# Mixer of a two-block network: the last conditioning blocks as a thread of their own, the first two parts of the output product as one, masked scans, and early priorities anew

## The chip, the cores and the metric

The kernel runs on one core of a Trainium2 chip. The metric is the device time of one launch in microseconds (us). Before the change it is 1557.97 us, the median of 3 runs (1557.44 to 1559.53). The engines are named as the profile names them: PE (TensorE matmul), PEld (its weight load), DVE (VectorE), ACT (ScalarE), POOL (GpSimd) and SP (SyncE, which only issues transfers here).

## The reference, cut to what matters

There are 512 tokens with 1024 features. The first block is the one that the change touches:

```python
ada = silu(c) @ w_ada + b_ada                 # 1024 -> 6 x 1024
sh_m, sc_m, g_m, sh_f, sc_f, g_f = split(ada, 6)
h = rms_norm(x) * (1 + sc_m) + sh_m
proj = h @ w_in                               # 1792 columns for RWKV, 512 for S5
z = shift(proj[..., :1792]); u = proj[..., 1792:]
y_rwkv = rwkv7_time_mix(z, ...)               # 8 heads of 64, a recurrence over the tokens
y_s5 = s5_mix(u, ...)                         # state space, GLU product, norm
x = x + g_m * (concatenate([y_rwkv, y_s5]) @ w_out)
h = rms_norm(x) * (1 + sc_f) + sh_f
x = x + g_f * ((silu(h @ w_gate) * (h @ w_up)) @ w_down)
```

Two hybrid layers (latent attention, short convolution, window attention) follow. The change only reaches them through the numbers that order some of their weight loads.

## The kernel before

**Products.** A large product is made of parts of 128 output features by 512 tokens. Each factor of 32 bits is split into a high and a low half, and three matmuls (high by high, high by low, low by high) of 128x512 make one k-tile of 128 rows. The weights' high half (`whi`) comes from ACT, the low half (`wlo`) from POOL or DVE. A part's sum lies in one of the three PSUM banks named `mm`; the job's evacuation reads it and frees it.

**The order.** Nothing of the mixer's order stands in the code. `class Flow` (from L378) runs threads, which are Python generators that yield one operation at a time. `Flow.run` always emits the operation with the earliest planned start, to which the thread's number in the table `BIAS` (L73) is added; this fixes every engine's program. The large products of the mixer are one fill thread, `gemm_g` (L1776), which walks through the list `JOBS` (L74 to L76): `z` (14 tiles of `h @ w_in`), `g` (the GLU product), `x` (the S5 half of `w_out`, four k-tiles, 8 jobs), `A` (two conditioning groups), then the RWKV half of `w_out` as `a` (two k-tiles, 8 jobs), `b` and `c` (one k-tile each, 8 jobs each). `a`, `b`, `c` wait for `mix.backs` > 1, > 2, > 3, the number of finished pairs of heads. Each job of `x`, `a`, `b`, `c` ends with `evac_x` (L1840): one DVE operation `xres += g_m * sum`.

**RWKV.** It goes over four pairs of heads p = 0 to 3. For each there are `front_a` (L1162, elementwise work and eight scans of 64 tokens), `front_b`, `invert` (a triangular inverse by way of transfers on SP's queue), `solve`, `chain` and `norm`. `chain` (L1416) is eight serial steps on one state: two matmuls from `UV` into columns 128:192 of the PSUM bank `cz`, two DVE operations that make the new state `Z`, one matmul from `Z` into columns 0:128, one DVE addition that makes the next `UV`. The matmuls into `Y` are the outputs of the step. `norm` (L1458) normalises `Y` and splits the result into `mr` (high and low), the factor of `a`, `b` and `c`.

**Conditioning.** The 48 blocks of `w_ada` are 12 groups. `group_a` (L1626) sums a group by 8 matmuls 32x512 (`<-wa,cT`), an ACT copy (`ev`), four matmuls 128x1 and one addition into `ada`. Ten groups run early; groups 10 and 11 (`g_f`, needed at the end of the FFN) are the jobs `A`. `finish` (L1907) closes the mixer when all 12 groups are there.

Of the kernel before, what the change touches and what calls it, by code (L numbers as in the profile page):

```python
# [47 lines left out]
_CR_SIZES = [("maskA", 128), ("mx", 64), ("i64", 64), ("blk", 128), ("sel0", 64), ("sel1", 64)]  # L48
# [38 lines left out]
LBIAS = {"latents": -2.98, "rows": -0.79, "token": 1.41, "keys": 1.03, "swa_q": 0.91, "head_gates": -0.43, "conv": -0.42, "mla_q": -0.75, "mla_k": -0.52, "mla_s": -2.46, "mla_m": -2.11, "mla_e": 1.23, "mla_n": 2.12, "mla_t": 1.14, "mla_v": -2.74, "swa_s": -1.25, "swa_m": 0.19, "swa_e": -2.03, "swa_v": -1.32, "convert": -0.49, "products": 1.27}  # L87
# [13 lines left out]
def _consts():  # L101
# [3 lines left out]
    c["ones"] = np.ones((128, 1))  # L105
    c["blkc"] = (p[:, None] // 64 == np.arange(2)[None]).astype(float)
# [31 lines left out]
def _tiles(w, kt, n):  # L138
    K, N = w.shape
    return np.ascontiguousarray(w.reshape(kt, 128, N // n, n).transpose(2, 1, 0, 3))  # L140


def pack(i):
# [9 lines left out]
    o["wada"] = np.concatenate([o.pop("wss"), wr], 0)  # L153
# [20 lines left out]
    o["wout"] = _tiles(np.concatenate([g["w_out"][0][:512], g["w_out"][0][512:][p5]], 0), 8, 128)  # L174
# [951 lines left out]
class Mix:  # L1126
# [35 lines left out]
    def front_a(self, p):  # L1162
# [371 lines left out]
def mixer(X, top, stop):  # L1534
# [115 lines left out]

    def loada(i0, i1, pool_, queue, bufs):
# [1285 lines left out]
```

## Time and profile before

| | us |
|---|---|
| median of 3 runs | 1557.97 (1557.44 to 1559.53) |
| the profiled execution | 1560.24 |
| its span | 1558.5 |
| PE busy | 1469.8 (94%) |
| DVE busy | 860.4 (55%) |
| ACT busy | 653.4 (42%) |
| POOL busy | 533.5 (34%) |

The profiled execution is 2.27 us above the median and 1.74 us longer than its span. Its mean granted clock of TensorE is 0.986. The mixer is the stretch from 0 to some 450 us; what follows is the FFN and the two layers.

How to read the rows below: a row of the timeline has the start, the duration, engine, line, operation, output<-inputs, the shape and the count of instructions that it holds, and in brackets how long the engine was idle just before and what ended that. A matmul's duration reaches from its start to its modelled end, so neighbouring ones overlap; the distance of starts says what one costs.

### The profile page before, as it was taken

How to read it: one execution, taken by the hardware profiler on the slowest of the kernel's cores; microseconds unless marked ns; L12 is line 12 of the kernel's file. 1: busy time of each engine (PE TensorE's matmuls, PEld its weight loads, DVE VectorE, ACT ScalarE, POOL GpSimd, SP SyncE). 2: the span in 40 equal slices, each digit the busy share in tenths (PEclk: the TensorE clock that was granted, in tenths of full speed). 3: DMA queues.
4: the chain of work that ended last, by engine and by line, in shares of the span. 5: the costliest groups of instructions: out<-in, count | busy, mean ns of one | idle time of the engine just before them, and what ended most of it. 6: DMA issues, size and time to landing. Idle time of an engine off the chain costs nothing.

```text
span 1558.5 us, 23572 instructions
## 1 busy us (share of the span) xinstructions
PE 1469.8 (94%) x8772; PEld 1123.0 (72%) x8772; DVE 860.4 (55%) x2011; ACT 653.4 (42%) x1316; POOL 533.5 (34%) x498
## 2 busy tenths in 40 slices
PE   4998899998879999999999989999999989999998
PEld 2666676666457888888888867866778867876776
DVE  6858776784676222221126474455874475463882
ACT  3422643232144333333333565355554366356452
POOL 1112350330323333334442454532325354542332
PEclk9999999999999999999999999999999999999999
DMA  6874141232222223333332311321222311221213
GB/s 251 288 214 90 50 121 32 70 94 75 63 82 75 97 95 98 98 95 91 98 95 63 103 55 54 102 68 55 71 54 88 91 61 61 81 76 61 70 54 102
DMA packets 97684, 141.92 MB, mean 91 GB/s; under 512 B 40977, under 2 KB 44945, under 8 KB 97553
## 3 DMA queue, kind: packets, MB, share of 16 engines
q1 hardware_dynamic: 90512, 120.46, 25.6%
q0 software_dynamic: 5760, 18.88, 3.9%
q8 instruction: 69, 1.13, 0.3%
q10 hardware_dynamic: 1296, 1.07, 0.2%
q14 instruction: 47, 0.38, 0.1%
HBM read 135.39 MB, written 4.98 MB: 90 GB/s over the span
## 4 chain that ended last, share of the span: by engine, by line
PE 74%; DVE 15%; ACT 4%; issue 2%; DMA 2%; POOL 1%; SPq 0%; ACTq 0%; DVEq 0%; POOLq 0%
PE mm L255 54%; PE rp L255 10%; PE rp L553 2%; PE O L255 2%; PE rq L255 2%; PE acc L255 2%; PE cz L255 1%; DVE wlo L236 1%; DVE sc L236 1%; DVE sq L236 1%; DVE P L249 1%; DVE qp L236 1%; POOL wlo L236 1%; DVE cy L252 1%; ACT qp L233 1%
## 5 line engine op out<-in xcount | busy, mean ns | idle before, releaser
L236 POOL TENSOR_TENSOR wlo<-wraw,whi 128x512 fp32r<-128x512 f32 (+2 forms) x300 | 379.6, 1267 | 766.4 <-ACT whi L233 731.1
L233 ACT ACTIVATE whi<-wraw 128x512 fp32r<-128x512 f32 (+2 forms) x392 | 239.1, 613 | 429.9 <-PE mm L255 300.7
L255 PE MATMUL mm<-hhi,wlo 128*128 128x512 f32 x920 | 368.4, 400 | 6.1 <-DVE wlo L236 6.1
L255 PE MATMUL mm<-hhi,whi 128*128 128x512 f32 x920 | 368.7, 401 | 1.7 <-DVE ca L236 1.0
L255 PE MATMUL mm<-hlo,whi 128*128 128x512 f32 x920 | 368.0, 400 | 0.0
L255 PEld LDWEIGHTS mm<-hhi,wlo 128*128 128x128 f32 x920 | 175.1, 190 | 49.5 <-DVE wlo L236 8.1
L255 PEld LDWEIGHTS mm<-hlo,whi 128*128 128x128 f32 x920 | 174.7, 190 | 44.0 <-issue 9.6
L255 PEld LDWEIGHTS mm<-hhi,whi 128*128 128x128 f32 x920 | 174.9, 190 | 42.6 <-issue 7.5
L236 DVE TENSOR_TENSOR wlo<-wraw,whi 128x512 fp32r<-128x512 f32 (+1 forms) x92 | 73.9, 804 | 113.7 <-ACT whi L233 102.9
L255 PE MATMUL mm<-ylo,whi 128*128 128x512 f32 x224 | 89.2, 398 | 1.6 <-POOL ylo L236 1.6
L255 PE MATMUL mm<-yhi,whi 128*128 128x512 f32 x224 | 89.7, 400 | 0.0
L255 PE MATMUL mm<-yhi,wlo 128*128 128x512 f32 x224 | 89.6, 400 | 0.0
L255 PE MATMUL mm<-ahi,whi 128*128 128x512 f32 x176 | 69.3, 394 | 0.0
L255 PE MATMUL mm<-ahi,wlo 128*128 128x512 f32 x176 | 69.0, 392 | 0.0
L255 PE MATMUL mm<-alo,whi 128*128 128x512 f32 x176 | 68.3, 388 | 0.0
L553 DVE CUSTOM_DVE_ANT_0 P<-rp,c,nsq 128x128 f32<-128x128 f32 (+1 forms) x64 | 34.2, 549 | 45.4 <-PE rp L255 41.3
L252 DVE SCALAR_TENSOR_TENSOR xres<-mm,ada,xres 128x512 f32<-128x512 f32 x40 | 29.7, 747 | 48.3 <-PE mm L255 48.1
L252 DVE SCALAR_TENSOR_TENSOR g<-th,mm 128x512 f32<-128x512 f32 x21 | 14.4, 687 | 70.6 <-PE mm L255 70.6
L252 DVE SCALAR_TENSOR_TENSOR th<-th,mm 128x512 f32<-128x512 f32 x20 | 13.7, 687 | 69.9 <-ACT th L233 69.9
L236 DVE TENSOR_TENSOR xres<-xres,mm 128x512 f32<-128x512 f32 x48 | 32.5, 681 | 35.0 <-PE mm L255 34.8
L255 PEld LDWEIGHTS mm<-ylo,whi 128*128 128x128 f32 x224 | 42.1, 188 | 12.5 <-POOL ylo L236 2.3
L255 PEld LDWEIGHTS mm<-yhi,wlo 128*128 128x128 f32 x224 | 42.0, 188 | 10.1 <-issue 1.1
(548 smaller groups left out, 2632.1 us busy)
## 6 DMA issues: line engine op xcount, KB each, us to landing
wraw<-in_w2m SPq DMA_DIRECT2D x124, 256.0 KB, 2.7
wa<-in_wada SPq DMA_DIRECT2D x40, 512.0 KB, 4.9
wraw<-in_wo SPq DMA_DIRECT2D x48, 256.0 KB, 2.7
wraw<-in_wgate SPq DMA_DIRECT2D x44, 256.0 KB, 2.7
wraw<-in_wup SPq DMA_DIRECT2D x44, 256.0 KB, 2.8
wraw<-in_wdown SPq DMA_DIRECT2D x40, 256.0 KB, 2.7
wraw<-in_wz POOLq DMA_DIRECT2D x24, 256.0 KB, 3.2
wa<-in_wada POOLq DMA_DIRECT2D x8, 512.0 KB, 3.7
```

Of the source, the lines that this page charges most:

```text
L233: return self.act.activation(out=out, in_=in_, func=func, **kw)
L236: return (eng or self.dve).tensor_tensor(out=out, in0=a, in1=b, op=op)
L249: return self.dve.tensor_scalar(out=out, in0=a, scalar1=s1, scalar2=s2, op0=op0, **kw)
L252: return self.dve.scalar_tensor_tensor(out=out, in0=a, scalar=s, in1=b, op0=op0, op1=op1)
L255: return self.pe.matmul(out, lhsT=lhsT, rhs=rhs, start=start, stop=stop)
L553: ins = fn(*args, **kw)
```

## The change

1. **`condb`, a new thread.** The jobs `A` go. The last 8 blocks of `w_ada` (40 to 47) are laid out anew, so that one block holds 128 outputs of `g_f`. Each is 8 matmuls 32x128 into columns 192:448 of the PSUM bank of the chain (`cz`), an ACT copy `evb` of 128x256, two matmuls 128x1 into columns 448 and 449, and two DVE additions of 128x1. The thread starts with `back_room`, where the loads of these blocks start too, and `finish` waits for 18 parts.
2. **`x` and `a` are one job.** A job `x` takes six k-tiles into one PSUM sum: four of S5 (`ms`), then two of RWKV (`mr`). The second part waits for `mix.backs` > 1. The rows of `w_out` are laid out S5 first. Eight evacuations `evac_x` go.
3. **Masked scans.** Per pair, eight scans of 128x64 become two of 128x256; a constant `keep`, zero at each multiple of 64, restarts the sum.
4. **Numbers.** The table `BIAS` is new nearly throughout, `JOBS` has another order of `z`, `g`, and the threads that load and convert weights for the layers get a number of their own (-0.28).

```diff
-BIAS = {... "solve": -1.29, "chain": -0.17, "norm": 0.63, "evac": -0.15, ... "fill": (-0.64, -1.41, 0.62, 1.6)}
+BIAS = {... "solve": -0.25, "chain": -0.39, "norm": -0.76, "evac": -0.14, ... "condb": 0.6, "late": 1.34, "fill": (-0.83, -5.66, 1.65, 3.61)}
...
-JOBS += [("x", m) for m in (0, 1, 2, 3, 4, 5, 6, 7,)] + [("A", m) for m in (10, 11,)] + [("a", m) for m in (0, 1, 2, 3, 4, 5, 6, 7,)]
+JOBS += [("z", m) for m in (1, 6, 9, 10, 2, 11, 3, 7,)] + [("x", m) for m in (0, 1, 2, 3, 4, 5, 6, 7,)]
...
-        one = C("ones").to_broadcast([128, 64])
-        for c in range(8):
-            yield o(dve.tensor_tensor_scan, L[:, ch(c)], one, L[:, ch(c)], 0.0, op0=ALU.mult, op1=ALU.add)
+        for a in (L[:, 0:256], L[:, 256:T]):
+            yield o(dve.tensor_tensor_scan, a, R("keep"), a, 0.0, op0=ALU.mult, op1=ALU.add)
...
+    def condb():
+
+        cz = pools["cz"]
+        for b in range(40, 48):
+            yield lambda: ("a", b) in first
+            wa = first.pop(("a", b)).rearrange("p a f -> p (a f)")
+            for k in range(KD):
+                q, n = slice(32 * (k % 4), 32 * (k % 4) + 32), 192 + 128 * (k // 4)
+                yield o(MM, cz[q, n:n + 128], cT[:, k:k + 1].to_broadcast([128, 32]), wa[:, k * 128:(k + 1) * 128])
+            st["la"] += 1
+            ev = pools["b"].tile([128, 256], F32, name="evb", tag="evb", bufs=1)
+            yield o(ACT, ev, cz[:, 192:448], scale=1.0 / 32.0)
+            for n in range(2):
+                yield o(MM, cz[:, 448 + n:449 + n], ev[:, n * 128:(n + 1) * 128], C("ones"))
+            yield o(X.ADD, ada[:, b:b + 1], cz[:, 448:449], V("bada", b, 1))
+            yield o(X.ADD, ada[:, b:b + 1], cz[:, 449:450], ada[:, b:b + 1])
+            st["adas"] += 1
...
-              "x": lambda m: (A["wout"][m][:, 4:8], 4), "a": lambda m: (A["wout"][m][:, 0:2], 2),
+              "x": lambda m: (A["wout"][m][:, 0:6], 6),
...
+                if kind == "x" and k0:
+                    yield lambda: mix.backs > 1
...
-        pools["wa"] = pools["b"]
         flow.spawn(loada(4 * NG0, 48, pools["b"], ADAQ(nc), NWA), BIAS["loada"])
+        flow.spawn(condb(), BIAS["condb"])
...
-        yield lambda: st["summed"] > KD and st["adas"] == 12
+        yield lambda: st["summed"] > KD and st["adas"] == NG0 + 8
```

**What moves on PE inside chain(0).** The rows are PE's program from the second step of the first pair's chain on. `RP`, `UV`, `mR`, `BKt`, `At` and `Z` are the chain's tiles, `hhi`/`hlo` with `whi`/`wlo` a job `z`. First the program before:

```order
L255 MATMUL Y<-Z_2082,RP 64x128
L255 MATMUL Y<-UV,mR 64x64 x2
L255 MATMUL mm<-hlo,whi_2225 128x512
L255 MATMUL mm<-hhi,wlo_2226 128x512
L255 MATMUL cz<-Z_2083,At 64x128
L553 MATMUL rp<-c_68,zv 128x128 x4
L553 MATMUL rp<-c_68,zv 64x128
L255 MATMUL mm<-hhi,whi_2225 128x512
L255 MATMUL cz<-UV,BKt 64x64 x2
```

And the same chain after:

```order
L257 MATMUL Y<-Z_2122,RP 64x128
L257 MATMUL Y<-UV,mR 64x64 x2
L257 MATMUL cz<-c_68,evb 128x1 x2
L257 MATMUL cz<-Z_2123,At 64x128
L257 MATMUL cz<-wa,cT 32x128 x5
L257 MATMUL cz<-UV,BKt 64x64 x2
L257 MATMUL Y<-Z_2123,RP 64x128
L257 MATMUL Y<-UV,mR 64x64 x2
L257 MATMUL cz<-wa,cT 32x128 x3
L257 MATMUL cz<-Z_2122,At 64x128
```

Between the steps stood a matmul or two of `z` and transposes of the next pair's front; now three blocks of `condb` (41 to 43) stand there, in pieces of 5 and 3 matmuls, in the bank that the chain's DVE operations read. Of the other five, block 40 stands in solve(0) and 44 to 47 between front_b(1) and solve(1). The chain itself has moved ahead of some 12 matmuls of `z`.

**What moves on PE in chain(3).** These are the middle steps of the last pair's chain before (`wa` is the job `A`):

```order
L255 MATMUL cz<-Z_2082,At 64x128
L255 MATMUL mm<-wa,cT 32x512 x2
L255 MATMUL cz<-UV,BKt 64x64 x2
L255 MATMUL Y<-Z_2082,RP 64x128
L255 MATMUL Y<-UV,mR 64x64 x2
L255 MATMUL cz<-Z_2083,At 64x128
L255 MATMUL cz<-UV,BKt 64x64 x2
```

And after:

```order
L257 MATMUL cz<-Z_2122,At 64x128
L257 MATMUL mm<-mr,whi_3905 128x512
L257 MATMUL mm<-mr,wlo_3906 128x512
L257 MATMUL mm<-mr,whi_3905 128x512 x2
L257 MATMUL mm<-mr,wlo_3906 128x512
L257 MATMUL cz<-UV,BKt 64x64 x2
L257 MATMUL Y<-Z_2122,RP 64x128
L257 MATMUL Y<-UV,mR 64x64 x2
L257 MATMUL mm<-ms,whi_4017 128x512 x2
L257 MATMUL mm<-ms,wlo_4018 128x512
L257 MATMUL mm<-ms,whi_4017 128x512 x2
L257 MATMUL cz<-Z_2123,At 64x128
```

Matmuls of the joined `x` (from `ms` and `mr`), some 30 in all, now stand in the gaps of this chain, which held 7 pieces of `A` or nothing.

**What moves on PE behind chain(3).** Before, 42 matmuls `mm<-mr` stand between the transposes of norm(2) and those of norm(3) (`rq<-c_68,ws`); the last of them and norm(3) read:

```order
L255 MATMUL mm<-mr,whi_4139 128x512 x2
L255 MATMUL mm<-mr,wlo_4140 128x512
L553 MATMUL rq<-c_68,ws 128x128 x4
L255 MATMUL mm<-mr,whi_4158 128x512
L255 MATMUL rq<-z,g_137 128x512
```

After, norm(2) is done ahead of chain(3), and 21 matmuls of the last two jobs `x` stand between the chain's end and norm(3):

```order
L257 MATMUL mm<-mr,whi_4118 128x512 x2
L257 MATMUL mm<-mr,wlo_4119 128x512
L257 MATMUL mm<-ms,whi_4182 128x512 x2
L257 MATMUL mm<-ms,wlo_4183 128x512
L257 MATMUL mm<-ms,whi_4182 128x512 x2
L257 MATMUL mm<-ms,wlo_4183 128x512
L257 MATMUL mm<-ms,whi_4182 128x512 x2
L257 MATMUL mm<-ms,wlo_4183 128x512
L257 MATMUL mm<-ms,whi_4182 128x512
L555 MATMUL rq<-c_68,ws 128x128 x4
L257 MATMUL rq<-z,g_137 128x512
```

On DVE, norm(3) no longer stands behind norm(2)'s end and among eight evacuations `xres`; those of the last jobs come after it. From the FFN on, the programs differ by swaps of two or three neighbours.

## Rows read from the trace of the kernel before

**Rows 1.** The page: busy time by engine, and the chain that ended last.

```profile
PE 1469.8 (94%) x8772; PEld 1123.0 (72%) x8772; DVE 860.4 (55%) x2011; ACT 653.4 (42%) x1316; POOL 533.5 (34%) x498
...
PE 74%; DVE 15%; ACT 4%; issue 2%; DMA 2%; POOL 1%; SPq 0%; ACTq 0%; DVEq 0%; POOLq 0%
```

**Rows 2.** Windows: stretch, length, busy per engine (PE, PEld, DVE, ACT, POOL), clock, DMA.

```profile
260.00:280.00 20.00, 20.00 (x302) 14.43 (x302) 15.11 (x48) 8.13 (x14) 3.63 (x4) 1.00 0.06 16
...
340.00:360.00 20.00, 18.59 (x336) 15.22 (x335) 15.40 (x36) 6.89 (x14) 1.83 (x3) 1.00 0.40 70
360.00:380.00 20.00, 18.32 (x310) 12.75 (x305) 7.17 (x19) 3.55 (x7) 1.81 (x3) 1.00 0.15 39
380.00:400.00 20.00, 16.70 (x132) 8.82 (x131) 11.03 (x43) 1.23 (x2) 2.66 (x5) 1.00 0.40 131
400.00:420.00 20.00, 18.81 (x86) 10.51 (x84) 13.38 (x29) 4.91 (x10) 5.97 (x9) 0.91 0.06 20
```

**Rows 3.** Timeline of PE, steps of chain(3) with and without `A`.

```profile
392.45 0.43 PE L255 MATMUL cz<-Z,At 128*64 128x128 f32 x2 [0.24 <-DVE Z L252]
392.82 1.05 PE L255 MATMUL mm<-wa,cT 128*32 128x512 f32 x4
...
394.81 0.43 PE L255 MATMUL cz<-Z,At 128*64 128x128 f32 x2 [0.23 <-DVE Z L252]
...
399.02 0.43 PE L255 MATMUL cz<-Z,At 128*64 128x128 f32 x2 [0.25 <-DVE Z L252]
...
400.87 0.43 PE L255 MATMUL cz<-Z,At 128*64 128x128 f32 x2 [0.24 <-DVE Z L252]
...
402.29 1.91 PE L255 MATMUL mm<-wa,cT 128*32 128x512 f32 x2
```

**Rows 4.** Timeline of PE, chain(1): its first step and its last matmul.

```profile
277.96 0.34 PE L255 MATMUL cz<-UV,BKt 128*64 128x64 f32 x4
...
278.79 0.40 PE L255 MATMUL mm<-hlo,whi 128*128 128x512 f32 x1
279.03 0.40 PE L255 MATMUL mm<-hhi,wlo 128*128 128x512 f32 x1
279.36 0.43 PE L255 MATMUL cz<-Z,At 128*64 128x128 f32 x2
...
295.00 0.45 PE L255 MATMUL Y<-UV,mR 128*64 128x64 f32 x4
```

**Rows 5.** Timeline of PE, from the end of chain(3) to the mixer's last sum.

```profile
405.25 0.49 PE L255 MATMUL Y<-UV,mR 128*64 128x64 f32 x4
...
408.50 0.95 PE L255 MATMUL mm<-c,ev 128*128 128x1 f32 x8
...
422.81 0.66 PE L553 MATMUL rq<-c,ws 128*128 128x128 f32 x4 [1.39 <-DVE ws L236]
...
433.18 1.01 PE L255 MATMUL mm<-mr,whi 128*128 128x512 f32 x2 [0.25 <-DVE xres L252]
...
448.37 1.87 PE L255 MATMUL mm<-c,sq 128*128 128x1 f32 x8 [4.93 <-DVE sq L236]
```

**Rows 6.** Timeline of DVE, the beginning and the end of norm(3).

```profile
410.82 0.68 DVE L553 TENSOR_REDUCE lnm<-Y 128x8 f32<-128x512 f32 x1
...
422.06 0.69 DVE L236 TENSOR_TENSOR ws<-ws,rsy 128x512 f32<-128x512 f32 x1
...
432.95 0.68 DVE L236 TENSOR_TENSOR mr<-ws,mr 128x512 fp32r<-128x512 f32 x1
```

**Rows 7.** Groups of DVE from 100 to 460 us, count, busy and mean of one in ns.

```profile
L252 DVE SCALAR_TENSOR_TENSOR xres<-mm,ada,xres 128x512 f32<-128x512 f32 x32 | 23.7, 746 | 2.8 <-PE mm L255 2.6
L252 DVE SCALAR_TENSOR_TENSOR Z<-Z,Pt,cz 64x64 f32<-64x64 f32 x48 | 13.4, 279 | 12.8 <-PE cz L255 12.0
...
L553 DVE TENSOR_TENSOR_SCAN w<-c,w 128x64 f32<-128x64 f32 x32 | 6.3, 269 | 0.1
L553 DVE TENSOR_TENSOR_SCAN sc<-rt,sc 128x512 f32<-128x512 f32 x4 | 5.7, 1473 | 0.0
```

More of the change, by code (lines that the diff above doesn't have):

```diff
@@ L72 @@
 FILLMIN, FILLOFF = 3032, 0.6
-BIAS = {"s5": -2.95, "fronta": -0.54, "frontb": -0.1, "invert": 1.54, "solve": -1.29, "chain": -0.17, "norm": 0.63, "evac": -0.15, "glu": -0.35, "conv": -0.28, "prep": -2.48, "w1p": -2.37, "wcp": 0.14, "wcd": 0.78, "toep": -0.79, "tw": 3.05, "x0": -3.3, "conv0": -1.6, "gemm0": 2.41, "loada0": -0.44, "load0": -1.44, "cond": -1.01, "loada": -1.83, "late": -0.0, "fill": (-0.64, -1.41, 0.62, 1.6)}
-JOBS = [("z", m) for m in (0, 13, 8,)] + [("g", m) for m in (0, 1, 2, 3,)] + [("z", m) for m in (5, 6, 9, 1, 2, 10, 11, 7, 3,)]
-JOBS += [("x", m) for m in (0, 1, 2, 3, 4, 5, 6, 7,)] + [("A", m) for m in (10, 11,)] + [("a", m) for m in (0, 1, 2, 3, 4, 5, 6, 7,)]
+BIAS = {"s5": -2.18, "fronta": -0.47, "frontb": -0.04, "invert": 1.65, "solve": -0.25, "chain": -0.39, "norm": -0.76, "evac": -0.14, "glu": -0.38, "conv": 0.54, "prep": -2.71, "w1p": -3.05, "wcp": 1.7, "wcd": 1.87, "toep": -0.62, "tw": 5.02, "x0": -3.54, "conv0": -1.33, "gemm0": 4.2, "loada0": 0.33, "load0": 1.78, "cond": -1.22, "loada": -0.67, "condb": 0.6, "late": 1.34, "fill": (-0.83, -5.66, 1.65, 3.61)}
+JOBS = [("z", m) for m in (0, 13, 8,)] + [("g", m) for m in (0, 1,)] + [("z", m) for m in (5,)] + [("g", m) for m in (2, 3,)]
+JOBS += [("z", m) for m in (1, 6, 9, 10, 2, 11, 3, 7,)] + [("x", m) for m in (0, 1, 2, 3, 4, 5, 6, 7,)]
 JOBS += [("b", m) for m in (0, 1, 2, 3, 4, 5, 6, 7,)] + [("c", m) for m in (0, 1, 2, 3, 4, 5, 6, 7,)]
@@ L1762, in mixer @@
             continue
-        if kind == "A":
-            parts.append((g, None, 0, 0))
-            continue
         src, K = source[kind](m)
@@ L1768, in mixer @@
     tail, tail_st = {}, ExitStack()
-    W.parts += [(src, (min(4, K), 128), LOADQ(nc), LOENG(X)) for g, src, k0, K in parts if K]
+    W.parts += [(src, (min(4, K - k0), 128), LOADQ(nc), LOENG(X)) for g, src, k0, K in parts]
     if stop not in ("h", "s5", "rwkv", "x1"):
@@ L1783, in gemm_g @@
             st["kind"] = kind
-            if kind == "A":
-                yield lambda: st["evac"] > g - 2
-                ps = X.mmt()
-                yield from group_a(m, ps, pools["wa"])
-                yield lambda: st["evac"] == g
-                st["evac"] += 1
-                continue
             single = kind in "bc"
-            for k in range(min(4, K)):
+            for k in range(min(4, K - k0)):
                 if single:
@@ L1801, in gemm_g @@
                     hi, lo = {"z": lambda: (hhi, hlo), "g": lambda: (s5t.glu["zh"], s5t.glu["zl"]),
-                              "x": lambda: (s5t.ms[:, 0], s5t.ms[:, 1])}.get(kind, lambda: (mixr()[:, 0], mixr()[:, 1]))()
-                kk = {"b": 2, "c": 3}.get(kind, k0 + k)
-                last = single or kk == K - 1
+                              "x": lambda: (s5t.ms[:, 0], s5t.ms[:, 1])}.get("m" if kind == "x" and k0 else kind, lambda: (mixr()[:, 0], mixr()[:, 1]))()
+                kk = {"b": 2, "c": 3}.get(kind, k if kind == "x" else k0 + k)
+                last = single or k0 + k == K - 1
+                if kind == "x" and k0:
+                    yield lambda: mix.backs > 1
                 for a, b in ((whi, hi), (whi, lo), (wlo, hi)):
-                    yield o(MM, ps, a[:, k], b[:, kk], (single or kk == 0) and a is whi and b is hi, a is wlo and last)
+                    yield o(MM, ps, a[:, k], b[:, kk], (single or k0 + k == 0) and a is whi and b is hi, a is wlo and last)
                 if last:
@@ L2913, in load_c2 @@
         yield Flow.op(nc.sync.dma_start, c2, X.A["c2"])
+    for th in flow.live:
+        if th[0].__name__ in ("load", "convert"):
+            th[2] = LBIAS["weights"]
     flow.spawn(load_c2(), 0.0)
```

18 lines of the change are left out of this document (10 added, 8 removed).

## The prediction

> **What bounds the kernel now.** I read the page first: PE is busy in 94% of the span, and 74% of the chain that ended last is PE's own work, 15% DVE's [rows 1]. So a change in the mixer pays only by taking matmuls off PE, or by filling the time in which PE stands and waits. The windows say where that time is: in chain(1), where matmuls of `z` stand between the steps, PE is busy in all 20 us, but from 340 us on it loses 1.41, 1.68, 3.30 and 1.19 us of each 20, and in the last of these windows the granted clock is 0.91 [rows 2]. The timeline shows the cause. A step of the chain with nothing between takes 1.85 us (399.02 to 400.87), with a piece of `A` between 2.36 us (392.45 to 394.81) [rows 3]; chain(1), with 29 matmuls of `z`, takes 17.5 us for eight steps [rows 4]. Two neighbouring matmuls of a fill start 0.24 us apart (278.79 to 279.03) [rows 4], so the 29 are 6.9 us and the step's own matmuls (17.5 - 6.9) / 8 = 1.33 us. An unfilled step thus hides some 0.5 us of fill. Behind chain(3) come 42.6 us (405.74 to 448.37) that end in a wait of 4.93 us for the last squares [rows 5].
>
> All terms are differences against the profiled execution, 1560.24 us; its 2.27 us above the median belong to the run, so I take the same differences from the median, 1557.97 us.
>
> **Part 1, the jobs `A` go.** In before they are eleven pieces and two sums. Seven pieces stand in steps of chain(2) and chain(3) and cost 2.36 - 1.85 = 0.51 us each, 3.6 us. The one at 402.29 took 1.91 us at the low clock [rows 2, 3], of which the step hides 0.5: 1.4 us. Three stand outside at 0.97 each (as at 392.82, less the overlap with its neighbour): 2.9 us. The sums from `ev` are 0.95 each [rows 5]: 1.9 us. Together -9.8 us.
>
> **Part 1, `condb` comes.** A piece of one or two matmuls 32x512 costs 0.97 us; at 128 columns a quarter, so eight matmuls lie between 0.5 us (when four of them run beside each other) and 1.0 us. Two matmuls 128x1 are half of the 0.95. A block is thus 1.0 to 1.5 us, and I take 1.1, since at `A` one matmul and two took the same time: 8 x 1.1 = +8.8 us (8.0 to 12.0).
>
> **Part 1, the shared bank.** No row of before shows a second user in the chain's bank, so this term is bounded. The chain's DVE operations (`Z` 279 ns, `UV` 290 ns [rows 7]) read columns 0:192 of the bank in which `condb` writes, copies by ACT and adds by DVE. If each of these accesses has to wait for the one before, whatever its columns, a block that stands inside a chain puts into the loop a copy, two matmuls and two additions, one behind another, and the DVE additions are queued ahead of the next `UV`, for which PE's next two matmuls wait. Three blocks (41 to 43) stand in chain(0). From below: nothing, if the accesses pass each other. From above: two whole steps a block, 2 x 1.85 = 3.7 us [rows 3], 11.1 us in all. I take 1.6 us a block, a little under one step, since a block has one round of PE to ACT to PE to DVE where a step has PE to DVE twice: +4.7 us. Of the other five blocks I cost the wait for the copy at nothing, because three matmuls of `z` (0.7 us) stand between the copy and the sum in four of them; without that cover it is up to 0.75 us a block.
>
> The Trainium skill (PSUM — Partial Sum Buffer, "PSUM bank collisions raise a hardware error") speaks against this edit: it asks that accesses of different engines to a bank be kept apart by bank and quadrant of partitions, not by address, so separate columns don't help. By that rule the term is not nothing but somewhere between my 4.7 us and the 11.1 us above; no row of before shows it either way.
>
> **Part 2, `x` and `a` as one.** The number of matmuls stays. Eight evacuations of 746 ns [rows 7] leave DVE, 6.0 us. DVE is not the bound; PE's waits for it in the last third are short, so I count 1 us of the 6: -1.0 us (0 to -3). What counts is where the matmuls stand. Thirty go into chain(3). Unfilled, and without `A`, it would take 8 x 1.85 = 14.8 us; filled 8 x 1.33 + 30 x 0.24 = 17.8 us. So 7.2 us of work costs 3.0 us there: -4.2 us. Some 23 more stand in the gaps of solve(2) and solve(3), where PE stands 3.1 us between 340 and 380 us [rows 2]: -2.5 us (0 to -3.1). In return the second part of an `x` needs the split of pair 1's `mr` directly behind norm(1); 12 matmuls less are in front of it, some 2.8 us of cover for a path of about 4 us (an estimate: from norm(3)'s transposes at 422.81 to the end of its split at 433.63, 10.8 us, less nine evacuations of 0.746 among it, leaves 4.1 [rows 5 to 7]): +1.2 us. In solve(2) a row of DVE operations stands ahead of one that PE waits for: +0.4 us.
>
> **Part 2, the end of the mixer.** In before, norm(3) starts on DVE at 410.82, 5.1 us after the chain's last matmul ends at 405.74, because norm(2) is still under way, and to the transposes at 422.81 six evacuations lie among it [rows 5, 6]. Its own length is from 410.82 to 422.75, less 6 x 0.746: 7.4 us. In after it begins at once, with 21 matmuls of `x` (5.0 us) beside it. Then 30 matmuls of `x` and `b` at 0.24 and the transposes, or 12 evacuations at 0.746 = 9.0 us, whichever is longer: 9.6 us with the transposes' start. Then `c` and the last sum as before, from 433.18 to 448.37 [rows 5]: 15.2 us. Together 32.2 us, against 42.6. Of these 10.4 us, 15 matmuls fewer (3.6) are counted in chain(3), `A` (1.9) in part 1, and norm(2)'s transposes (1.6) only move; 3.3 us are gained waits: -3.3 us. The mean clock of 0.91 (part of the stretch at 1.2 GHz, the rest at 2.4) follows the stretch in which PE was busiest least, 16.70 of 20 us [rows 2]; a filled chain should hold 1.00, worth 0.09 x 18.8 = 1.7 us, of which 0.9 is in the 1.91 above: -0.8 us.
>
> **Switches.** From `z` to the chain's matmul it is 0.33 us (279.03 to 279.36) instead of 0.24 [rows 4], 0.09 for each change of kind. The new order has 50 more changes, 4.5 us; about half stand where PE waits anyway: +2.2 us (0 to 4.5).
>
> **Part 3, scans.** Eight scans of 269 ns overlap; two half as wide as the 1473 ns of a 128x512 scan are 1.5 us against 1.57 to 2.2 us [rows 7]. Only the first pair's is waited for: -0.2 us (0 to -0.5).
>
> **Part 4, numbers.** Up to 120 us and from the FFN on only neighbours swap places: 0, with 2 us either way.
>
> The sum: -9.8 + 8.8 + 4.7 - 1.0 - 4.2 - 2.5 + 1.2 + 0.4 - 3.3 - 0.8 + 2.2 - 0.2 = -4.5 us. The forecast is 1557.97 - 4.5 = 1553.5 us. Its own range, with the terms between their near ends, is 1550.5 to 1557.
>
> **The rivals.**
>
> *The bank costs nothing.* The chain's DVE operations and `condb` pass each other; the 4.7 us fall away: -9.2 us, 1548.8 us. For it: chain(0) has long waits in which the copy could lie. Against it: the two additions on DVE stand ahead of `UV` in any case.
>
> *PE was full anyway.* The matmuls moved into the chains are missing where they stood, and new gaps open there: chain(0), which loses its `z` and front work, runs at 1.85 a step as chain(3) does now, and solve(0) with it. Then the 4.2 and 2.5 us come back as new waits: about +2, or 0 with a part of them, 1558 us. For it: the order gives the same work to PE and 2 us more of it (switches); against it: 48 matmuls of `z` still stand behind chain(0).
>
> *Slower: two rounds for each block.* By the rule that separate columns don't help, each block in chain(0) waits for a `Z` before its matmuls, makes the next `Z` wait for its copy, and makes `UV` wait for its additions: two steps, 3.7 us for three blocks, and the other five wait for their copy, 0.75 each. That is 11.1 + 3.8 = 14.9 in place of 4.7: -4.5 + 10.2 = +5.7, 1563.7 us. It decides from 2.9 us a block with the five at 0.75 (8.7 + 3.8 - 4.7 - 4.5 = +3.3). The rule of the skill named above is on its side.
>
> **How the numbers follow.** Forecast 0.45, bank free 0.20, PE full anyway 0.18, slower 0.17. 0.2% is 3.1 us, about what a measurement can tell from no change. Of the forecast's own range some 0.30 of 0.45 lies below 1554.9; with the free bank faster has 0.50. Same gets the rest of the forecast and most of "full anyway": 0.31; slower 0.19. The range goes from 1547.5 to 1562: below it lies a third of the free bank, above it most of the slower case, together 0.2.
>
> **What would show it.** Right: chain(0) longer than 17.5 us with waits of PE's `cz` matmuls for DVE and ACT around `evb`; chain(3) near 17.8 us with no wait over 0.2 us; norm(3)'s transposes 7 to 8 us behind the chain's last matmul; the last sum some 32 us behind it; clock 1.00 at 400 us. Wrong: chain(0) at 15 us or above 22 us; a wait above 2 us at the first `mr` matmul of `x`, or of `b` for its evacuations; a difference in the FFN or the layers of more than 2 us, which no term here has.

## The result, and the profile after

The change made the kernel slower. Before, the median is 1558.75 us (4 runs, 1557.44 to 1560.87); after, 1579.37 us (4 runs, 1574.41 to 1589.44), a ratio of 1.0135 with the interval 1.0107 to 1.0164. The forecast was 1553.5 us with a range up to 1562: wrong in sign, and the time lies outside the range.

The profiled execution of after is its slowest, 1589.44 us. Its page, to be held against [rows 1]: the span, the busy times, the chain that ended last.

```profile
span 1587.7 us, 23792 instructions
...
PE 1489.0 (94%) x8884; PEld 1140.8 (72%) x8884; DVE 856.2 (54%) x1993; ACT 655.3 (41%) x1322; POOL 537.1 (34%) x498
...
PE 58%; DVE 8%; ACT 3%; issue 1%; DMA 0%; POOL 0%; ACTq 0%; DVEq 0%; POOLq 0%; SPq 0%
```

DVE has 18 instructions less and PE 112 more, as the change says: it adds 56 matmuls, and the profile has two records for a matmul of 32 bits (the eight of a block stand in it as x16). PE is busy 19.2 us longer, though it was given little more to do: that is in the main the clock, as the windows show (columns as in [rows 2]), two of before and then four of after.

```profile
180.00:200.00 20.00, 19.25 (x151) 14.85 (x149) 15.81 (x46) 10.17 (x19) 5.93 (x7) 1.00 0.17 54
240.00:260.00 20.00, 19.76 (x189) 13.62 (x189) 9.29 (x31) 5.55 (x12) 1.81 (x2) 1.00 0.20 41
```

```profile
180.00:200.00 20.00, 18.40 (x124) 13.16 (x120) 11.17 (x30) 7.29 (x15) 3.64 (x4) 0.74 0.20 39
...
240.00:260.00 20.00, 17.18 (x148) 11.79 (x145) 6.89 (x26) 1.37 (x3) 1.07 (x2) 0.71 0.51 125
260.00:280.00 20.00, 19.12 (x82) 11.79 (x81) 10.29 (x32) 5.05 (x9) 4.20 (x5) 0.61 0.12 40
...
340.00:360.00 20.00, 15.52 (x71) 10.38 (x71) 15.16 (x36) 7.30 (x13) 6.30 (x8) 0.83 0.43 153
```

Before, the granted clock is 1.00 in all four stretches ([rows 2] for the last two); after, it is 0.61 to 0.83, and 0.61 means most of the stretch at 1.2 GHz and the rest at 2.4. The counts of matmuls don't compare, since other work stands there: of the 302 records of before from 260 to 280 us, 256 are small ones of 64x64, where after does its chain(0). I cut the run at three places that both kernels have: the first matmul of the GLU product (`mm<-zs`), the last matmul of `z` (`mm<-hhi` in the mixer) and the mixer's last sum (`mm<-c,sq`). "Idle" is the sum of PE's idle times in the timeline, "half" the time at the lower clock level, from windows of 2 us (4 us times one minus the clock of each). The idle time of the second stretch leaves out the wait that ends in the last sum itself (4.93 us before, 4.27 after; in e2 it stands ahead of a block and is counted), and its windows reach a little past that sum. Each row is one profiled execution; the kernels from e1 on are the experiments below.

| kernel | its time | GLU to last `z`: length, idle, half | last `z` to last sum: length, idle, half | last sum to end |
|---|---|---|---|---|
| before | 1560.2 | 139.1, 3.7, 0.0 | 141.4, 14.6, 7.0 | 1111.9 |
| after | 1589.4 | 173.7, 15.1, 47.8 | 139.8, 16.3, 15.1 | 1108.4 |
| after again (e14) | 1573.6 | 163.0, 17.0, 17.0 | 139.8, 16.4, 15.4 | 1102.7 |
| e1 | 1566.9 | 155.0, 18.5, 13.7 | 140.9, 15.2, 23.0 | 1104.2 |
| e2 | 1575.0 | 148.5, 11.9, 6.8 | 153.8, 19.3, 26.7 | 1104.7 |
| e3 | 1588.3 | 174.5, 18.2, 27.4 | 137.8, 14.5, 23.2 | 1107.7 |
| e4 | 1589.9 | 150.2, 14.4, 9.7 | 164.0, 25.4, 24.4 | 1109.2 |
| e5 | 1578.8 | 160.7, 17.2, 10.2 | 144.1, 18.5, 17.2 | 1106.9 |
| e6 | 1577.4 | 152.3, 9.0, 17.1 | 150.0, 17.8, 6.7 | 1106.2 |
| e11 | 1580.2 | 162.7, 14.6, 13.6 | 146.2, 12.3, 23.9 | 1104.2 |
| e13 | 1557.0 | 138.9, 3.4, 0.0 | 140.0, 14.8, 4.4 | 1109.5 |
| e16 | 1552.5 | 120.1, 4.2, 0.0 | 158.5, 16.2, 12.8 | 1106.2 |
| e19 | 1596.7 | 170.5, 15.0, 34.2 | 155.1, 19.1, 52.2 | 1103.2 |
| e20 | 1601.2 | 161.0, 11.1, 6.8 | 171.4, 18.1, 80.2 | 1102.2 |
| e21 | 1567.2 | 121.1, 6.5, 6.8 | 176.8, 19.1, 25.4 | 1101.4 |

The GLU product starts at 167.9 us before and 167.5 us after; nothing is lost ahead of it. Behind the last sum after is shorter, by 3.5 us in the first profile and 9.2 in e14. Timeline of PE there, before and then after:

```profile
475.45 0.38 PE L255 MATMUL mm<-c,rows 2*128 2x1 f32 x2 [2.04 <-ACT rows L233]
```

```profile
506.68 0.38 PE L257 MATMUL mm<-c,rows 2*128 2x1 f32 x2
```

Before waits 2.04 us for ACT at this place, 27 us behind the last sum, and 6.8 us at half clock follow (476 to 484 us); after has neither. How the 3.5 and the 9.2 us come about in full is not shown.

Against before, the loss stands in one stretch, GLU to last `z`: 34.6 us more in the profiled run, 23.9 in the repetition. `condb` accounts for about 8 us of it (163.0 in e14, 155.0 without the blocks in e1; the blocks now stand there, while `A` stood behind the last `z`), less 3.1 us (an estimate) of matmuls of a front that moved behind. The rest is 11 to 13 us of new waits and the clock.

The waits of PE in after from 100 to 500 us, by what was waited for (us in total, times, longest):

```profile
PE rq L555 <- DVE ws L238: 7.0, 3, 4.5
...
PE rq L257 <- DVE sc L238: 2.6, 1, 2.6
...
PE rp L257 <- DVE rk L254: 1.9, 1, 1.9
...
PE cz L257 <- ACT evb L235: 0.8, 1, 0.8
```

The largest stands behind the last `z`, outside the stretch that lost. The timeline of PE there, and of DVE in the same 10 us (start, length, in brackets the idle time before and its releaser):

```profile
341.25 0.40 PE L257 MATMUL mm<-hhi,wlo 128*128 128x512 f32 x1
341.57 1.13 PE L257 MATMUL rp<-z,w2a 64*128 64x512 f32 x4
342.63 0.73 PE L257 MATMUL mm<-ms,whi 128*128 128x512 f32 x2
...
345.26 0.39 PE L257 MATMUL mm<-ms,wlo 128*128 128x512 f32 x1
350.12 0.63 PE L555 MATMUL rq<-c,ws 128*128 128x128 f32 x4 [4.48 <-DVE ws L238]
```

```profile
342.11 0.69 DVE L238 TENSOR_TENSOR mr<-ws,mr 128x512 fp32r<-128x512 f32 x1 [4.41 <-ACT mr L235]
342.72 0.68 DVE L555 TENSOR_REDUCE lnm<-Y 128x8 f32<-128x512 f32 x1
...
349.29 0.69 DVE L238 TENSOR_TENSOR ws<-ws,rsy 128x512 f32<-128x512 f32 x1
```

The norms run one after another. The last act of norm(0) splits its result into `mr`, which shares a buffer with the `hlo` that every `z` reads; so the split (342.11) has to wait for the last `z` (341.25) by way of ACT's copy into `mr`, and norm(1)'s first operation stands behind it on DVE. Norm(1) then needs 7.3 us until its `ws` (342.72 to 349.98), and PE has only one `rp` group and 12 matmuls of `x` for that, 4.1 us (341.57 to 345.65). It then stands for 4.48 us. Before, a front and some 50 matmuls of `x` stood beside this norm, and its transposes waited 0.41 us:

```profile
333.66 0.65 PE L553 MATMUL rq<-c,ws 128*128 128x128 f32 x4 [0.41 <-DVE ws L236]
```

Within the stretch that lost, the largest wait is the one for the sum of the S5 norm. Timeline of PE, before and then after:

```profile
191.75 1.05 PE L255 MATMUL rq<-c,sc 128*128 128x1 f32 x8
```

```profile
214.45 1.87 PE L257 MATMUL rq<-c,sc 128*128 128x1 f32 x8 [2.63 <-DVE sc L238]
```

Before, the sum starts 3.7 us after the last matmul of the GLU product (188.04), and PE has work all that time. After, it starts 5.8 us after it (208.67), of which PE has work for 3.2. So the cover is only a little thinner; the path is longer, since on DVE an operation of another thread (`M`, 1.78 us from 210.94 on) stands ahead of the norm's own, which takes 1.75 us instead of 1.02.

### The profile page after: what moved, and what is told of

Read it like the earlier page. It is cut to its first block, busy times and chain, and to the rows that moved or that the text cites. A ratio compares the mean times of both kernels' runs of the same rounds, so it can differ in the third digit from the quotient of the medians.

```text
span 1587.7 us, 23792 instructions
## 1 busy us (share of the span) xinstructions
PE 1489.0 (94%) x8884; PEld 1140.8 (72%) x8884; DVE 856.2 (54%) x1993; ACT 655.3 (41%) x1322; POOL 537.1 (34%) x498
## 4 chain that ended last, share of the span: by engine, by line
PE 58%; DVE 8%; ACT 3%; issue 1%; DMA 0%; POOL 0%; ACTq 0%; DVEq 0%; POOLq 0%; SPq 0%
PE mm L257 47%; PE rp L257 7%; PE O L257 3%; PE rp L555 2%; DVE wlo L238 1%; DVE P L251 1%; DVE qp L238 1%; DVE cy L254 1%; DVE sq L238 1%; ACT qp L235 1%; ACT sq L235 1%; DVE qp L254 0%; DVE xres L254 0%; ACT whi L235 0%; ACT P L235 0%
## 5 line engine op out<-in xcount | busy, mean ns | idle before, releaser
L254 DVE SCALAR_TENSOR_TENSOR g<-th,mm 128x512 f32<-128x512 f32 x21 | 14.5, 689 | 69.1 <-PE mm L257 69.0
L254 DVE SCALAR_TENSOR_TENSOR th<-th,mm 128x512 f32<-128x512 f32 x20 | 13.7, 687 | 70.2 <-ACT th L235 70.2
L254 DVE SCALAR_TENSOR_TENSOR xres<-mm,ada,xres 128x512 f32<-128x512 f32 x32 | 23.6, 749 | 50.3 <-PE mm L257 50.1
```

Of the source, the lines that this page charges most:

```text
L254: return self.dve.scalar_tensor_tensor(out=out, in0=a, scalar=s, in1=b, op0=op0, op1=op1)
```

## The experiments

Two theories stood against each other first: **the blocks** (`condb` in chain(0) lengthens the chain by its accesses to the shared bank and lets the clock fall) and **the order** (the new order leaves PE without cover at the fronts and norms, whatever `condb` does).

**e1: after's order without the blocks.** `condb` issues nothing but its weight loads, its eight outputs are set to one; every other instruction keeps its place.

```
-        ins = fn(*args, **kw)
...
+        if self.cur.__name__ != "condb":
+            ins = fn(*args, **kw)
...
+        pool.memset(ada[:, 40:48], 1.0)
```

> The changed kernel with every engine's order as it is, but the instructions of the last eight conditioning blocks left out (their outputs are set to one; their loads stay). Theory A, the blocks in the chain's bank are what costs: in the changed kernel's profile chain(0) takes 29 us (242.6 to 271.6), nearly all of it at a granted clock of 0.50 (1.2 GHz); without the blocks its steps are 1.3 to 1.9 us, 15 us or less at 1.00, so the time falls by 12 to 16 us, to 1563 to 1567 us. Theory B, the new numbers' order is what costs: the stalls of 1.9 us before the first rk matmul (176 us), 2.6 us before the S5 norm's sum (214 us) and 4.5 us before norm(1) (350 us) and the low clock behind each stay, and the time falls by the blocks' own 8 to 10 us at most, to 1570 us or above.

Measured: 1572.04 us (1566.93 to 1576.42), ratio 1.0086 (1.0053 to 1.0119). So, by the medians, all eight blocks, work and waits together, cost 7 to 9 us (the intervals of the ratios with and without them just overlap, at 1.011); 13 us of loss remain without them. The waits for `sc` (2.6), `rk` (1.9) and norm(1) (4.5) stand unchanged in its trace. The blocks are a third. The rest is left to the order and the other edits, the joined products and the scans, which the next runs take apart.

**e2: the blocks behind the chains,** planned anew.

```
-            yield lambda: ("a", b) in first
+            yield lambda: ("a", b) in first and mix.chained > 3
```

> The changed kernel with the eight blocks held back until chain(3) is over; the planner orders anew from solve(0) on. Theory A: the chains stay free of them, chain(0) runs at a clock of 1.00 in 18 us with its fill, and the time is 1560 to 1566 us (the blocks cost 8 to 10 us at the end, among products that wait for DVE anyway). Theory B: the stalls at 176 and 214 us stay, 1570 us or above.

Measured: 1575.18 us, ratio 1.011 (1.0078 to 1.0141). The first stretch gets 14.5 us shorter than in the repetition of after, the second 14 us longer: what leaves chain(0) is paid behind it. The waits for `rk` (1.87) and `sc` (2.62) stay, as the second theory has it.

**e3: after with the old numbers** (the old `BIAS` and `JOBS`, `condb` at 0.6; the -0.28 stays).

```
-BIAS = {... "solve": -0.25, "chain": -0.39, "norm": -0.76, ...}
+BIAS = {... "solve": -1.29, "chain": -0.17, "norm": 0.63, ...}
```

> The changed kernel with the priorities and the order of products z and g of the kernel before (0.6 for the blocks' thread); blocks 41 to 43 still stand in chain(0). Theory A: chain(0) still takes above 22 us and its clock falls; the time stays at 1570 us or above. Theory B: the stalls at 176 and 214 us go, 1560 to 1565 us.

Measured: 1587.83 us (1586.19 to 1588.47), ratio 1.0187 (1.0166 to 1.0207). The second theory, which had 1560 to 1565 us, is wrong here: the wait for `sc` is gone, but the one for `rk` is 3.4 us, others come, and the old numbers with the new operations are worse than the new ones. The first theory's forecast (chain(0) above 22 us, 1570 us or above) came, with a chain(0) of 24.5 us; but chain(0) was 24.1 and 29.6 us long in after too, so it doesn't explain the 5 to 8 us that this kernel is slower than after by the medians. So the new numbers are not to blame as such; what they cost depends on the operations.

**e5: `x` and `a` apart again,** the rest as after.

```
-              "x": lambda m: (A["wout"][m][:, 0:6], 6),
+              "x": lambda m: (A["wout"][m][:, 0:4], 4), "a": lambda m: (A["wout"][m][:, 4:6], 2),
```

> The changed kernel with the first two parts of the output product as two jobs again; the order is the same up to the last z matmul (342 us). If joining them costs time (the second part of a job waits for norm(1) while it holds a bank, which leaves 12 matmuls as fill ahead of norm(1)), the time falls by 5 us or more. By theories A and B, which see the loss ahead of it, it stays within 3 us of the changed kernel's 1574 to 1589 us, with the three stalls as they are.

Measured: 1585.68 us, ratio 1.0184 (1.0147 to 1.0221). Joining them is no loss. By the medians it gains 3 to 6 us (after: 1579.37 and, in e14, 1582.46), but the intervals overlap and the order behind the last `z` is another, so a gain is not shown. Its chain(0) runs at the higher clock but for 3.4 us, so the blocks' price can be read there, against e1. Timeline of PE, the first and the last matmul of chain(0)'s eight steps, in e1 and then in e5:

```profile
235.93 0.34 PE L257 MATMUL cz<-UV,BKt 128*64 128x64 f32 x4
...
250.19 0.45 PE L257 MATMUL Y<-UV,mR 128*64 128x64 f32 x4
```

```profile
236.75 0.34 PE L257 MATMUL cz<-UV,BKt 128*64 128x64 f32 x4
...
241.65 0.61 PE L257 MATMUL cz<-c,evb 128*128 128x1 f32 x4 [0.79 <-ACT evb L235]
...
259.30 0.45 PE L257 MATMUL Y<-UV,mR 128*64 128x64 f32 x4
```

14.71 us without blocks (1.84 a step, the forecast's unfilled 1.85), 23.00 with three; at most 1.7 us of the 8.3 are the lower clock (half of 3.4), so a block lengthens the chain by some 2.2 us, its own matmuls included. The Trainium skill (PSUM — Partial Sum Buffer, "PSUM bank collisions raise a hardware error") asks that a bank be guarded by semaphores whatever the address in it. The trace of after has such waits between different columns: at 267.88 us DVE's `Z` has waited 0.51 us for ACT's `evb`, which it doesn't read. The blocks with these waits cost 2.2 us each. The rival that followed the rule had 3.7 beside the matmuls.

**e4: before with the new numbers,** no other edit of its operations. The diff is e3's `BIAS` the other way round, with the new `JOBS` and the -0.28 for the layers' weight threads.

> The kernel before with the priorities and the order of products z and g of the changed kernel, all else as before (conditioning groups among the products, the output product in four parts, eight scans). If the new order of the early work is what brings the waits, PE waits 2 us or more before the S5 norm's sum and before norm(1)'s transposes here too, the clock falls behind them, and the time is 1566 us or above. If it is the new thread and the joined products, within 4 us of the kernel before.

Measured: 1591.95 us, ratio 1.0215 (1.0179 to 1.025). With the old operations the new numbers lose even more, 33 us, with 25.4 us of idle time and 24.4 at half clock in the second stretch. The waits of PE from 100 to 500 us (us in total, times, longest) are those of after, for the norms and for the S5 norm's sum:

```profile
PE rq L554 <- DVE ws L237: 14.7, 3, 6.0
...
PE rq L256 <- DVE sc L237: 2.3, 1, 2.3
```

So these waits come with the numbers and not with the new operations.

**e6 and e13: the masked scans alone,** in two ways. e6 puts them into before and lets the order be planned anew; e13 keeps before's order, with the wide scan where the first of its four narrow ones stood.

```
-        for c in range(8):
-            yield o(dve.tensor_tensor_scan, L[:, ch(c)], one, L[:, ch(c)], 0.0, op0=ALU.mult, op1=ALU.add)
+        for a in (L[:, 0:256], L[:, 256:T]):
+            yield o(dve.tensor_tensor_scan, a, R("keep"), a, 0.0, op0=ALU.mult, op1=ALU.add)
```

> The kernel before with the masked scans alone; the planner orders anew, since it gives two scans 1.37 us and eight 2.27. From the traces two scans take 1.27 us where eight took 1.57: 0.3 us a pair, of which the first pair's is on the path: -0.3 us, same as the kernel before within 2 us. A larger change in either direction would be the planner's new order, not the scans.

> The kernel before with the masked scans put in at the places of the first and the fifth of the eight scans, every engine's order otherwise as before (the planner still plans eight). If the 17.5 us that the masked scans cost with a new order are the new order's, this is the kernel before within 1.5 us (two scans take 1.27 us for 1.57). If the masked scans themselves cost (a slower operation, another landing of the constants), it is slower by 5 us or more.

Measured: e6 1576.3 us, ratio 1.0105 (1.008 to 1.0129); e13 1559.0 us, ratio 1.0003 (0.9991 to 1.0016). The waits of PE from 160 to 460 us, e6 and then e13, show a part of it, 6 us (us in total, times, longest); another are 17 us at half clock ahead of the last `z`, where e13 has none:

```profile
PE rp L256 <- DVE rk L253: 3.6, 2, 3.4
PE rp L256 <- DVE w L253: 3.4, 2, 1.9
```

```profile
PE rp L256 <- DVE rk L253: 0.7, 2, 0.4
```

The edit itself is worth nothing. That six operations a pair fewer stand in the plan moves the order, and the new one costs 17 us. This is the cleanest pair of the study: same instructions, two orders, 17 us.

**e11, e12 and e18: waits filled with work.** Matmuls of two constants, whose result is overwritten, stand ahead of matmuls that wait: 50 in after at five waits, 20 in before at two, and those 20 in e13; the order is otherwise kept.

```
+        if eng == "PE" and out.tensor.name in self.pre:
+            X, ps, n = self.pre.pop(out.tensor.name)
+            for _ in range(n):
+                ins = X.MM(ps[:, 0:128], X.C("ident"), X.C("ident"))
```

> The changed kernel in its own order, with 50 extra matmuls 128x128 of constants put before five instructions at which PE waits: 6 before the first pair's rk matmul, 9 before the S5 norm's sum, 16 before norm(1)'s transposes, 5 before norm(3)'s, 14 before the block's last sum. Their results are overwritten by the instruction behind them. By the theory that a wait costs twice, once by itself and once by the low clock that follows it, they fill waits and no low clock follows them: the stretches behind 176, 214, 350 and 481 us (in the changed kernel's profile 34 us at a clock of 0.50, worth 17 us) go at a clock of 1.00, the one in chain(0) stays, and the time falls by 6 to 14 us below the changed kernel's median of 1579. If the low clock has another cause, or the waits alone are the loss, the time stays within 3 us or grows by the extra matmuls that do not fit into a wait.

> The kernel before in its own order, with 4 extra matmuls 128x128 of constants before norm(3)'s transposes and 16 before the block's last sum (waits of 1.39 and 4.93 us). By the same theory the stretch at a clock of 0.50 behind 446 us (6.8 us, worth 3.4 us) goes, and the time falls by 2 to 4 us. If the low clock has another cause: within 1 us of the kernel before.

> The kernel before in its own order with the masked scans in place and the 20 extra matmuls of constants before norm(3)'s transposes and the block's last sum. If both do what the single edits promise (0.3 us for the first pair's scans; 2 to 4 us for the stretch of low clock behind the last sum), it is 1.5 to 4 us faster than the kernel before.

Measured: e11 1578.4 us, ratio 1.0105 (1.0066 to 1.0144); e12 1558.14, ratio 0.9987 (0.9973 to 1.0001); e18 1559.0, ratio 1.0001 (0.9989 to 1.0013). In e12 the lower clock behind the last sum is gone and the time is the same. In e11 it is gone behind the first two filled waits (1.00 from 170 to 230 us) and stays in chain(0) as in e14 (7 us); from 348 us on there are 17 us at half clock, where e14 has 7. No gain is shown; whether the lower clock is a cause of its own or goes with short supply of work, these runs don't settle.

**e14: after again,** unchanged.

> The changed kernel once more, unchanged. Its four runs so far go from 1574.4 us at a mean granted clock of 0.982 to 1589.4 at 0.970, 1.25 us for each thousandth of the clock. If the low clock is what scatters them, these runs lie on the same line, 1571 to 1590 us, and the profile of a run near 1578 has less than the 63 us at a clock of 0.50 between 160 us and the last sum that the first profile has.

Measured: 1582.46 us (1573.55 to 1585.72), ratio 1.0142 (1.0117 to 1.0168). The same instructions in the same order took 1573.6 us here and 1589.4 in the first profile, with about the same idle time (33.4 and 31.4 us in the two stretches). What differs is the clock; windows of e14, to hold against those of after above:

```profile
180.00:200.00 20.00, 17.90 (x132) 12.35 (x132) 13.60 (x36) 10.97 (x21) 5.50 (x6) 1.00 0.36 67
...
240.00:260.00 20.00, 16.45 (x126) 10.57 (x124) 7.42 (x28) 2.47 (x5) 3.00 (x5) 0.83 0.45 119
260.00:280.00 20.00, 17.47 (x101) 12.89 (x102) 16.18 (x43) 7.04 (x12) 5.65 (x6) 0.91 0.12 37
```

Over the whole span the mean clock is 0.982 in the run of 1574.41 us and 0.970 in that of 1589.44: 15 us for 0.012, 1.25 us for each thousandth. Before had 0.986 in its profile. Carried on to there, an estimate from these two runs, after would take 1569.4 (a line through all eight runs of after gives 1567.5): about half of the 20.6 us is clock, the other half waits and work.

**e16 and e21: before with one number moved by 0.03,** no other edit.

```
-BIAS = {... "chain": -0.17, ...}
+BIAS = {... "chain": -0.14, ...}
...
-BIAS = {... "glu": -0.35, ...}
+BIAS = {... "glu": -0.32, ...}
```

> The kernel before with one number of the table changed a little: the chain's priority from -0.17 to -0.14. Nothing else changes, no work is added; the planner orders some 1,300 rows of PE anew. If the loss of the changed kernel and of its parts is that of leaving an order whose waits had all found cover, this is slower by 5 to 20 us, with idle time and low clock between the GLU product and the last z matmul, where the kernel before has 3.7 us and none. If an order of the planner is as good as its neighbour, it is within 3 us of the kernel before.

> The kernel before with the GLU thread's priority from -0.35 to -0.32; some 1,800 rows of PE in a new order, the work the same. The nudge of the chain's number gave 1553.9 us against 1558.9. If orders next to each other scatter by 10 us or more, as the masked scans' new order (1576.3) says, this is anywhere from 1552 to 1580; within 2 us of the kernel before would say that the order matters little by itself.

Measured: e16 1553.92 us (1549.52 to 1558.58, 10 runs), ratio 0.9965 (0.9953 to 0.9977); e21 1567.18 us, ratio 1.006 (1.0037 to 1.0083). The same operations, in three orders that differ by 0.03 in one number, lie at 1553.9, 1558.9 and 1567.2 us. e16 beats both kernels, so the idea that every order but the old one loses has fallen. It moves `z` forward by 19 us, at no more idle time than before (4.2 against 3.7), pays most of it back behind (158.5 us to the last sum, where before has 141.4), and its end is not better covered. Of the 7.7 us between the two profiles, 5.7 stand behind the last sum, where before has the wait for `rows`. Windows of e16:

```profile
260.00:280.00 20.00, 19.21 (x117) 15.52 (x117) 16.21 (x52) 8.67 (x15) 10.15 (x11) 1.00 0.28 72
...
420.00:440.00 20.00, 11.94 (x33) 6.59 (x32) 14.13 (x31) 5.18 (x9) 1.68 (x2) 0.74 0.12 40
```

**e19 and e20: the number of the norms.** One theory was that after's early norms (-0.76 instead of 0.63) put the waits there. e19 sets them back in after; e20 also lets a block run only while no chain is under way.

```
-BIAS = {... "norm": -0.76, ...}
+BIAS = {... "norm": 0.63, ...}
...
-            yield lambda: ("a", b) in first
+            yield lambda: ("a", b) in first and mix.chained == mix.solved
```

> The changed kernel with the norm thread's number put back alone (-0.76 to 0.63). Norm(0)'s transposes then stand behind the next pair's whole front instead of behind 20 z matmuls (4.7 us for DVE's 7.4), norm(1)'s behind solve(2) instead of 12 matmuls. Theory C, the covers are short because of this number: the waits of 2.5 and 4.5 us before them and the low clock behind go, and the time falls by 7 to 12 us below the changed kernel's 1580.7 (median of 8), to 1569 to 1574; blocks 41 to 43 stay in chain(0) and keep their 5 us. Theory D, the new structure has too little fill in any order: other waits take their place, 1577 us or above.

> As the run before, and a conditioning block starts only while no chain is under way. By theory C and the price of the shared bank (1.8 us for each of three blocks in chain(0)), another 5 us less, 1562 to 1569 us, at best the kernel before; by theory D 1575 us or above.

Measured: e19 1595.92 us, ratio 1.0238 (1.0207 to 1.0269); e20 1601.93 us, ratio 1.0302 (1.0259 to 1.0345). The theory has fallen: norm(1)'s 4.5 us are gone in e19, and 52 us at half clock now stand behind the last `z`. In e20 chain(0) is free of blocks, the first stretch has 11.1 us idle and 6.8 at half clock, and the second 80 us at half clock. So this number alone is not the cause. Both times fit the other expectation set there, that the new operations have too little fill in any order (1577 us or above); no run rules it out. The five orders of them with other numbers or places (after, e2, e3, e19, e20) lie between 1575.2 and 1601.9 us, and whether a better one exists was not searched.

## Why the prediction was wrong

**The bound: right.** PE sets the pace, and time is lost where it waits in the mixer.

**`A` goes, `condb` comes: near.** -9.8 and +8.8 were set; no run measures the -9.8. The blocks with all their waits cost 7 to 9 us (e1), where 8.8 and 4.7 for the bank, 13.5, were summed. In chain(0) 2.7 us a block were set (1.1 and 1.6), 2.2 were measured, 6.6 for the three. The other five thus cost some 0.5 to 2.5 us together where 5.5 were set: they lie in time that PE had. The term was too large by some 5 us, on the cautious side; the rival of two rounds for each block (3.7 beside the 1.1) didn't come. The sign set for "wrong", chain(0) above 22 us, did: it is 29.6 us in the profile of after and 24.1 in e14, of which the blocks are 6.6 on top of 14.7; the rest goes with the lower clock (0.60 over the 29.6 us). Its first and last matmul in after:

```profile
242.63 0.34 PE L257 MATMUL cz<-UV,BKt 128*64 128x64 f32 x4
...
271.58 0.69 PE L257 MATMUL Y<-UV,mR 128*64 128x64 f32 x4
```

**Chain(3) filled: right.** It was to be 17.8 us for eight steps with no wait over 0.2 us; it takes 18.6 us (426.06 to 444.69) at a clock of 1.00, and PE waits for nothing in it. (Before, this chain held four pieces of `A`, at 390.45, 392.82, 397.01 and 402.29, not the seven named with the change.)

**The end of the mixer: half right.** Norm(3)'s transposes were to come 7 to 8 us behind the chain, the last sum 32. Timeline of PE in after, the first and the last matmul of chain(3), the transposes, and the end:

```profile
426.06 0.34 PE L257 MATMUL cz<-UV,BKt 128*64 128x64 f32 x4
...
444.24 0.45 PE L257 MATMUL Y<-UV,mR 128*64 128x64 f32 x4
452.84 0.63 PE L555 MATMUL rq<-c,ws 128*128 128x128 f32 x4 [1.78 <-DVE ws L238]
...
471.02 0.73 PE L257 MATMUL mm<-mr,whi 128*128 128x512 f32 x2 [1.02 <-DVE xres L254]
...
475.18 1.22 PE L257 MATMUL mm<-mr,whi 128*128 128x512 f32 x2 [0.99 <-DVE xres L254]
...
481.09 1.87 PE L257 MATMUL mm<-c,sq 128*128 128x1 f32 x8 [4.27 <-DVE sq L238]
```

The transposes start 8.2 us behind the chain's end (444.69), the last sum 36.4 us. Norm(3) still has a wait of 1.78 us, since the matmuls beside it are fewer than its 7.4 us; the products then wait for their evacuations three times by 1 us. The clock of 1.00 that was forecast for 400 us is there; the 15 us at half clock from the last `z` on stand behind norm(1)'s wait (350 us) and at the last sum (from 474 us). The end was to be 10.4 us shorter, it is 6.2 (42.6 less 36.4).

**The scans: right.** -0.2 forecast, nothing measured with the order kept (e13).

**Joining `x` and `a`: no loss (e5), but its gains didn't come.** The waits to be gained in chains, solves and the end were summed at 10 us (4.2, 2.5, 3.3). Chain(3) did take its matmuls, but at norm(1) and the end the time was given back: idle time behind the last `z` is 16.3 us against 14.6. The forecast's terms for this stretch, `A` among them, come to some -17 us (an estimate: -20.0, and 3.1 for the front that moved in); measured is -1.6. So about as much of the miss stands behind the last `z` as ahead of it, where some +10 was summed (8.8, 4.7 and -0.2, less 3.1) and +23.9 measured in e14. No wait over 0.5 us stands at the first `mr` of an `x` (+1.2 was set), and no run separates the switches (+2.2) or the +0.4 in solve(2).

**"Part 4, numbers: 0, with 2 us either way": the step that failed.** It looked only up to 120 us and from the FFN on, where orders differ by neighbours. From 167 to 341 us the order is a new one, and no term of the sum stood for it. The stretch lost 11 to 13 us to waits and, in the profiled run, 48 us ran at half clock. What the runs showed in place of the 0: the new numbers alone cost 33 us on the old operations (e4) and by the medians gain 5 to 8 on the new ones (e3 against after); a new order of one set of instructions cost 17 (e6 against e13). From the FFN on it was not 0 either: one wait of 2 us went. At the two norms the order itself would have told: norm(1) stands on DVE behind a split that waits for the last `z`, and 12 matmuls of `x` (4.1 us with the `rp` group) cover its 7.3 us, which puts a wait of 3 us or more there before anything has run. For norm(0) 20 matmuls of `z`, 20 x 0.24 = 4.8 us, cover 7.4 us [rows 4 to 6]; PE waits 2.5 us for it in e14 and e1 (in the profile of after only 0.8, since the `z` there ran in part at the lower clock and so covered more). At the S5 norm's sum a count of matmuls would not have been enough, since its path on DVE had grown. The prediction's rival "PE was full anyway" named chain(0) and solve(0) as the place where gaps open, which was right in part (the waits for `rk` and `sc`, 1.9 and 2.6 us, lie ahead of them); but it priced them at what was gained elsewhere, +2 us in all, without counting them.

**The clock: mis-sized.** It entered with -0.8 us. It is worth about half of the loss, by the estimate from the runs of after above. That more gaps go with more of it is in the table (more idle and more half-clock time, the two stretches together, in all planned-anew kernels), but single rows break the rule: e16 has more of both than before and is faster, and e20's second stretch has less idle time than e4's and three times its time at half clock. What brings the clock down stays open.

**What stays open:** which property makes one order good, and whether the new operations have a good one at all. The kernels with an order planned anew scatter from 1553.9 to 1601.9 us, and neither the blocks' place nor the norms' number sorts them.

## What to carry to other kernels

Where a planner sets the order, an edit is two edits: the operations, and the order that follows from them. Test the edit once in the old order (e6 and e13: +17 us against nothing), and price the new order before running it: for each matmul that waits on another engine's chain of operations, count the matmuls that stand between that chain's start and it, and the other threads' operations within the chain. Such a count finds waits, not the time: e19 took both norm waits away and was slower. A nudge of one priority by 0.03 was worth -5 or +8 us here, as much as the -4.5 us that the edit's terms summed to; so a change that brings new numbers is to be compared with several orders of the kernel before, not with one.

## What the runs showed of the hardware

TensorE's clock falls not only behind waits. In before, at 1208 us, PE is busy without a gap; 24 records of one-column matmuls follow rows of wide ones, and the next wide matmul runs at 1.2 GHz. Timeline of PE, then a window (columns as in [rows 2]):

```profile
1208.53 0.39 PE L255 MATMUL mm<-hhi,wlo 128*128 128x512 f32 x1
1208.75 3.13 PE L255 MATMUL rp<-c,sq 128*128 128x1 f32 x24
1211.75 0.77 PE L255 MATMUL mm<-hhi,whi 128*128 128x512 f32 x1
1212.32 0.63 PE L255 MATMUL mm<-hlo,whi 128*128 128x512 f32 x1
1212.75 0.63 PE L255 MATMUL mm<-hhi,wlo 128*128 128x512 f32 x1
```

```profile
1210.00:1218.00 8.00, 8.00 (x29) 6.69 (x29) 6.60 (x35) 0.90 (x3) 0.61 (x1) 0.57 0.07 26
```

A matmul that started 0.23 us behind its neighbour before the sums (1208.30 to 1208.53) starts 0.43 us behind it after them (1212.32 to 1212.75), with no wait between. And the same program, in the same order, was granted 0.982 in one run and 0.970 in another, 1574.4 and 1589.4 us: of a kernel whose supply of work has gaps, a single run says little to 1%.
